# The output phase of the first token tiles woven into the third attention pair of the last block, with w_out in the place of the projection rows and weights

## The chip, the cores and the metric

One core of one Trainium2 chip runs the whole kernel. The metric is the device time of one execution in microseconds (us). Engines are named as in the profile: PE (TensorE), DVE (VectorE), ACT (ScalarE), POOL (GpSimd), SP (SyncE, which here issues the DMAs).

## The reference

One layer of a decoder trunk over 2048 tokens with 1024 channels, float32. The normalised input goes through one projection w_in whose columns feed three token mixers; their gated outputs are joined, projected by w_out and added to the input.

```python
h = rms_norm(x, norm_g) * (1 + scale) + shift
(ga_u, ga_v, ga_z, mb_q, mb_k, mb_v, mb_o, mb_z, mb_i, mb_f, sc_q, sc_k, sc_v, sc_z) = split(h @ w_in)
y_a = spatial_gating_branch(ga_u, ga_v, ...) * silu(ga_z)                  # 256 columns
h_b = mlstm_branch(conv(mb_q), conv(mb_k), mb_v, mb_i, mb_f)               # scan over 16 chunks of 128 tokens
y_b = sigmoid(mb_o) * rms_norm(h_b) * silu(mb_z)                           # 384 columns
y_c = stick_breaking_branch(rms_norm(sc_q), rms_norm(sc_k), sc_v) * silu(sc_z)   # 384 columns
out = x + gate * (concat([y_a, y_b, y_c]) @ w_out)

def stick_breaking_branch(q, k, v):        # 6 heads x 64, per block of 128 queries
    z = q @ k.T * scale
    log_not = where(strict, log_sigmoid(-z), 0.0)
    suffix = reverse_cumsum(log_not) - log_not
    a = where(strict, exp(log_sigmoid(z) + suffix), 0.0)
    return a @ v
```

The stick-breaking attention is causal, so a query tile i needs the i+1 key tiles up to itself. The mLSTM carries a state C from chunk to chunk.

## The kernel before, in words

Tokens are cut into 16 tiles of 128 and these into three blocks of 5, 5 and 6 tiles (BLOCKS). For a block the normalised, transposed rows hT stay in SBUF as a high and a low half (two float32r numbers whose sum is the float32), and every product with them is three matmuls: high by high, high by low, low by high. The weights wr are split in the same way; eight tiles of them make one set of 384 columns.

A block walks over three pairs of attention heads (p = 0, 1, 2 in the loop at the end of the kernel). For each pair `c_proj` projects q, k, v of the block's tiles, and `stick` runs the attention in units of up to four key tiles, each in four steps that lie one unit apart: `front` (two z matmuls, two sigmoids on ACT into bb and be, the running product of bb by a scan on DVE at L391, the product be at L395 on DVE and POOL in turn), `middle` (four PE transposes `at`, a cast on ACT at L408, the low half by a subtraction on DVE at L409), `back` (the av matmuls, L421) and `fin` (py, and the tile's 128 columns written to the DRAM scratch y_d). In the last block a pair is 44 units.

`interleave` runs a generator of fillers beside `stick`: other column sets of w_in, one `chunk` each (six tiles of 24 matmuls with 384 columns, 144 in all in the last block). They are bqk (q and k of the mLSTM), bg (its gates), cz, a (spatial gating) and bv (v of the mLSTM). In the last block pair 0 has bqk 0, bqk 1 and bg 0, pair 1 has bg 1, cz and a 0, pair 2 has a 1, and bv stands after the loop as `tail`; the gate scan `gating` and the mLSTM's chunk 0 (`first_chunk`) are mixed in. All results go to DRAM scratch (qkT_d, vb_d, gate_d, y_d).

What stands after `t0 += nb` is the output phase. It closes the pools of rows, weights and PSUM and opens its own: eight PSUM banks of five kinds, and w_out (`wst`, `wo`), which `split_wo` takes into high and low halves, eight tiles by two column halves. For each token tile i, `load` brings its parts back, `mlstm` does the chunk's scores, sums and the state's update (matmuls s, k, i, n, c and one DVE operation behind each), `mixed` normalises and gates, `turned` transposes y into yT, and `out_proj` does 48 matmuls `po` of 512 columns, multiplies by the gate (DVE, L967), adds x (POOL, L968) and stores. `weave` puts the steps of tile i+1 between the matmuls of tile i.

The order on each engine is made by the framework's scheduler from this program order and from priorities (`prio`; the sticks are ahead of the fillers by STK). Each engine then runs its own list in order, so an instruction that waits holds up all that stands behind it on its engine. The steps below speak of L296 to L298 (projection matmuls), L391, L395, L406 to L409, L421 (sticks), L640 (mLSTM weights by Exp on ACT), L863 and L864 (split of w_out), L914 (n), L957 to L959 (po).

Of the kernel before, what the change touches and what calls it, by code (L numbers as in the profile page):

```python
# [17 lines left out]
P = 128  # L18
# [14 lines left out]
def hybrid_block_kernel(ctx: ExitStack, tc: tile.TileContext, x, c, norm_g, w_ada, b_ada, w_in,  # L33
# [419 lines left out]
    def bqk_proj(t0, nb, half):  # L453
# [3 lines left out]
        for mm in range(3):  # L457
            m = half * 3 + mm
            for q in range(2):
# [9 lines left out]
                xb = tmp.tile([P, 64 * NBMAX + 3], F32, tag="xb", name=f"xb{m}_{t0}_{q}")  # L469
# [272 lines left out]
    def interleave(main, main_cost, side, side_cost):  # L742
# [14 lines left out]
        if side is not None:  # L757
            run(side)
# [48 lines left out]

    t0 = 0
    for b, nb in enumerate(BLOCKS):
# [7 lines left out]
        ]  # L817
        if b == 1:
            fillers[0] = (mix(fillers[0][0], 8, gate_gemv()), 3)
        if last:  # L820
            fillers[0] = (mix(fillers[0][0], 36, gating()), 3)
            fillers[1] = (mix(fillers[1][0], 14, first_chunk()), 3)
        for p in range(3):
# [4 lines left out]
            if p == 2 and not last:  # L828
                get_x(t0 + nb, 0)
                get_x(t0 + nb + 1, 1)  # L830
            interleave(stick(p, t0, nb), stick_cost(t0, nb), fillers[p][0], fillers[p][1] * chunk)
        tail = bv_proj(t0, nb)
        if last:
            run(tail)
        else:
# [9 lines left out]

    rs.close()
    lw.close()
    ps_ctx.close()
    pj_ctx.close()
    ld = ctx.enter_context(tc.tile_pool(name="ld", bufs=2))  # L850
    wk = ctx.enter_context(tc.tile_pool(name="wk", bufs=2, side="right"))
    wo_p = ctx.enter_context(tc.tile_pool(name="wo", bufs=1, side="right"))
    psS = ctx.enter_context(tc.tile_pool(name="psS", bufs=1, space=PSUM, side="right"))
    psN = ctx.enter_context(tc.tile_pool(name="psN", bufs=1, space=PSUM, side="right"))
    psK = ctx.enter_context(tc.tile_pool(name="psK", bufs=1, space=PSUM, side="right"))
    wo = [wo_p.tile([P, 2, D], F32R, tag=f"wo{k}", name=f"wo{k}") for k in range(KT)]

    wst = [ld.tile([P, 2, D], F32, tag=f"wst{kp}", bufs=1, name=f"wst{kp}") for kp in range(KT // 2)]

    def split_wo(k, n):  # L860
        cs = slice(n * 512, (n + 1) * 512)
        src = wst[k // 2][:, k % 2, cs]
        nc.scalar.copy(wo[k][:, 0, cs], src)  # L863
        (nc.gpsimd if k % 2 else nc.vector).tensor_tensor(wo[k][:, 1, cs], src, wo[k][:, 0, cs].bitcast(F32),  # L864
                                                          ALU.subtract)

    nds = {}
# [176 lines left out]
```

## Time and profile before

| what | us |
|---|---|
| median of the runs | 1480.47 |
| the profiled execution, its own time | 1480.27 |
| its span from first to last instruction | 1478.5 |
| last block, pair 0 (737 to 911 of the span) | 174 |
| last block, pair 1 (911 to 1084) | 173 |
| last block, pair 2 with bv (1084 to 1214) | 130 |
| output phase (1214 to the end) | 264.5 |

Times within the kernel are microseconds from the start of the span. The four stretches are cut where the sticks of a pair end on PE; a pair's `c_proj` lies at the stretch's start (that of pair 0 in part before it). Busy times of an engine are the union of its instructions; a busy PE is not PE at its peak, since matmuls are pipelined, so the pitch from one start to the next is used for its rate. PEclk is the share of TensorE's clock that was granted.

### The profile page before, as it was taken

The page shows a single profiled execution, that of the slowest core. Times are in us where ns is not written, and L with a number is a line of the kernel's source. Part 1 is how long each engine was busy: PE and PEld are TensorE (multiplying, and loading weights), DVE is VectorE, ACT ScalarE, POOL GpSimd, SP SyncE. Part 2 cuts the span into 40 slices and gives each one's busy share as a digit, 9 for nine tenths or more (in the row PEclk, how much of TensorE's full clock was granted, in tenths as well). Part 3 has the DMA queues.
Part 4 walks back from the last instruction along what each step waited for, and adds up shares of the span by engine and source line. Part 5 has one row for each costly group of instructions (what it writes and reads, how often), then busy time and mean ns, then how long its engine had stood idle before and what let it go on. Part 6 is the DMA issues. An engine that isn't in the chain of part 4 may idle for free.

```text
span 1478.5 us, 24942 instructions
## 1 busy us (share of the span) xinstructions
PE 1400.6 (95%) x8468; PEld 1302.7 (88%) x8468; DVE 1025.1 (69%) x1778; ACT 678.1 (46%) x1656; POOL 647.3 (44%) x1140
## 2 busy tenths in 40 slices
PE   4999999889999999999999899999999978999998
PEld 3789999879999999988899799989999867888887
DVE  6796555586894566588698975778778888444443
ACT  3365444444464355446367655555455655211210
POOL 4463554573443433455233353433344336534442
PEclk9999999999999999999999999999999998999999
DMA  9866766657635534625332343303432524555551
GB/s 319 305 203 216 249 213 190 207 187 240 203 114 194 175 114 137 213 98 184 114 117 78 104 148 131 104 27 107 158 100 74 190 89 128 185 152 159 171 156 57
DMA packets 187103, 233.19 MB, mean 158 GB/s; under 512 B 22714, under 2 KB 160344, under 8 KB 186976
## 3 DMA queue, kind: packets, MB, share of 16 engines
q1 hardware_dynamic: 186752, 231.59, 48.1%
q8 instruction: 67, 1.10, 0.3%
q14 instruction: 60, 0.49, 0.1%
q0 software_dynamic: 224, 0.02, 0.0%
HBM read 159.24 MB, written 72.31 MB: 157 GB/s over the span
## 4 chain that ended last, share of the span: by engine, by line
PE 68%; DVE 16%; DMA 5%; issue 4%; POOL 3%; ACT 3%; SPq 1%; DVEq 0%; POOLq 0%; ACTq 0%
DVE bb L391 6%; PE av L421 5%; PE pc L296 4%; PE pc L298 4%; PE at L406 4%; PE pc L297 4%; PE po L957 4%; PE po L959 3%; PE po L958 3%; PE pg L298 3%; PE pg L297 3%; PE pg L296 3%; PE pb L465 2%; PE pb L464 2%; PE z L378 2%
## 5 line engine op out<-in xcount | busy, mean ns | idle before, releaser
L391 DVE TENSOR_TENSOR_SCAN bb<-bb,bb 128x513 f32<-128x513 f32 x144 | 194.1, 1348 | 24.9 <-ACT bb L383 23.8
L395 POOL TENSOR_TENSOR be<-be,bb 128x512 f32<-128x512 f32 (+3 forms) x120 | 133.0, 1108 | 148.3 <-DVE bb L391 69.2
L409 DVE TENSOR_TENSOR aT<-at,aT 128x512 fp32r<-128x512 f32 (+3 forms) x240 | 142.7, 597 | 31.5 <-ACT aT L408 30.5
L421 PE MATMUL av<-aT,Vst 128*128 128x256 f32 x816 | 146.4, 296 | 15.0 <-DVE aT L409 12.1
L408 ACT CAST aT<-at 128x512 fp32r<-128x512 f32 (+3 forms) x240 | 127.1, 530 | 70.3 <-PE at L406 67.4
L383 ACT ACTIVATE bb<-z 128x512 f32<-128x512 f32 (+3 forms) x240 | 130.3, 544 | 54.5 <-PE z L379 44.2
L421 PEld LDWEIGHTS av<-aT,Vst 128*128 128x128 f32 x816 | 120.5, 192 | 27.0 <-DVE aT L409 19.2
L296 PE MATMUL pc<-wr,hT 128*128 128x384 f32 (+1 forms) x384 | 136.8, 358 | 7.6 <-DVE hT L290 5.7
L406 PE MATMUL at<-ident,be 128*128 128x128 f32 x816 | 132.8, 277 | 9.6 <-DVE Qst L351 4.5
L298 PE MATMUL pc<-wr,hT 128*128 128x384 f32 (+1 forms) x384 | 135.5, 353 | 1.6 <-DVE hT L290 1.5
L297 PE MATMUL pc<-wr,hT 128*128 128x384 f32 (+1 forms) x384 | 134.0, 349 | 0.0
L384 ACT ACTIVATE be<-z 128x512 f32<-128x512 f32 (+3 forms) x240 | 132.1, 550 | 0.0
L406 PEld LDWEIGHTS at<-ident,be 128*128 128x128 f32 x816 | 99.2, 142 | 19.0 <-DVE aT L409 8.0
L957 PE MATMUL po<-wo,yT 128*128 128x512 f32 x256 | 105.0, 410 | 0.3 <-ACT yT L946 0.3
L958 PE MATMUL po<-wo,yT 128*128 128x512 f32 x256 | 102.3, 400 | 1.9 <-DVE wo L864 1.9
L391 DVE TENSOR_TENSOR_SCAN bb<-bb 128x129 f32<-128x129 f32 (+3 forms) x96 | 86.9, 905 | 23.5 <-POOL bb L386 16.3
L959 PE MATMUL po<-wo,yT 128*128 128x512 f32 x256 | 101.5, 400 | 0.0
L382 POOL MEMSET bb<- 128x1 f32 x240 | 24.2, 101 | 168.4 <-DVE bb L391 118.1
L378 PE MATMUL z<-Kst,Qst 128*128 128x512 f32 (+3 forms) x240 | 92.7, 387 | 1.7 <-ACT be L384 1.6
L466 PE MATMUL pb<-hT,wr 128*128 128x320 f32 (+1 forms) x288 | 91.9, 324 | 2.4 <-DVE wr L190 2.4
L464 PE MATMUL pb<-hT,wr 128*128 128x320 f32 (+1 forms) x288 | 93.1, 324 | 0.6 <-DMA wr<-w_d 0.6
L465 PE MATMUL pb<-hT,wr 128*128 128x320 f32 (+1 forms) x288 | 92.2, 322 | 0.0
(272 smaller groups left out, 3905.2 us busy)
## 6 DMA issues: line engine op xcount, KB each, us to landing
wr<-w_d SPq DMA_DIRECT2D x160, 384.0 KB, 5.6
w_d<-wr SPq DMA_DIRECT2D x80, 384.0 KB, 3.5
wad<-in_w_ada_dram SPq DMA_DIRECT2D x8, 1024.0 KB, 6.8
xo<-in_x_dram SPq DMA_DIRECT2D x16, 512.0 KB, 3.7
out_dram<-o SPq DMA_DIRECT2D x31, 256.0 KB, 2.9
xt<-in_x_dram SPq DMA_DIRECT2D x15, 512.0 KB, 3.5
st<-in_w_in_dram SPq DMA_DIRECT2D x60, 128.0 KB, 3.7
wr<-w_d SPq DMA_DIRECT2D x16, 392.0 KB, 6.0
```

The source lines that it names most:

```text
L296: nc.tensor.matmul(ps, lhsT=hT[:, 0, k, cols], rhs=wt[k][:, 0, :W], start=k == 0, stop=False)
L297: nc.tensor.matmul(ps, lhsT=hT[:, 0, k, cols], rhs=wt[k][:, 1, :W], start=False, stop=False)
L298: nc.tensor.matmul(ps, lhsT=hT[:, 1, k, cols], rhs=wt[k][:, 0, :W], start=False, stop=k == KT - 1)
L384: nc.scalar.activation(be[:, :w], z[:, :w], AF.Sigmoid)
L391: nc.vector.tensor_tensor_scan(rev, rev, rev, carry.get((i, h), 1.0), ALU.mult, ALU.bypass)
L395: eng.tensor_tensor(be[:, :w], be[:, :w], bb[:, 1:w + 1], ALU.mult)
L406: nc.tensor.transpose(at[:, s, :], be[:, s * P:(s + 1) * P], ident)
L409: nc.vector.tensor_tensor(aT[:, :nb_, 1, :], at[:, :nb_, :], aT[:, :nb_, 0, :].bitcast(F32), ALU.subtract)
L421: nc.tensor.matmul(flat(av), lhsT=Vst[:, s0 + s, h, :], rhs=flat(aT[:, s]), start=(s0 + s == i), stop=(s0 + s == 0))
L957: nc.tensor.matmul(po, lhsT=yT[:, 0, k, :], rhs=wo[k][:, 0, cs], start=k == 0, stop=False)
L958: nc.tensor.matmul(po, lhsT=yT[:, 0, k, :], rhs=wo[k][:, 1, cs], start=False, stop=False)
L959: nc.tensor.matmul(po, lhsT=yT[:, 1, k, :], rhs=wo[k][:, 0, cs], start=False, stop=k == KT - 1)
```

## The change

The last block's fillers are dealt anew: pair 0 has bqk 0, bqk 1, bg 0 and bg 1, pair 1 has cz, a 0, a 1 and bv, four chunks each. Nothing of w_in is left for pair 2. Ahead of its sticks the pools of rows and weights are closed, w_out takes their place in SBUF, and the output phase itself, now a generator `output`, is the filler of the sticks of pair 2. `interleave` gives it up to 6 x 14500 ns of its own count of cost and, with `finish=False`, leaves the rest, which runs when the sticks have ended. Token tiles 0 to 5 and a part of 6 come before that end.

The buffers change with it. Until the sticks have ended the five kinds of PSUM tiles of `mlstm` share one bank (tag m) apart from the transposes, which use the sticks' `at` banks; afterwards s and n take the sticks' z banks and i the av bank. SBUF tiles of `mlstm`, `mixed`, `out_proj` and the staged w_out come from the six buffers t512 that the projections use too; gt, xt, vb use the buffers va and gu, xt, xb; the gate row lies in hscale. w_out is staged in pieces of 128 x 512. The computation is the same.

```diff
-    def interleave(main, main_cost, side, side_cost):
+    def interleave(main, main_cost, side, side_cost, finish=True):
...
-        if side is not None:
+        if side is not None and finish:
             run(side)
...
+    def open_out():
+        lw.close()
+        pj_ctx.close()
+        out_pools["o"] = ctx.enter_context(tc.tile_pool(name="psO", bufs=2, space=PSUM, side="right"))
+        out_pools["m"] = ctx.enter_context(tc.tile_pool(name="psM", bufs=1, space=PSUM, side="right"))
+        out_pools["ld"] = ctx.enter_context(tc.tile_pool(name="ld", bufs=2))
+        wo.extend(out_pools["ld"].tile([P, 2, D], F32R, tag=f"wo{k}", bufs=1, name=f"wo{k}") for k in range(KT))
+
+    def bank(kind, name):
+        pool, tag = {"s": (pz, "z"), "n": (pz, "z"), "i": (pav, "av")}.get(kind) if alone[0] and kind in "sni" else \
+            (pat, "at") if kind == "t" else (out_pools["m"], "m")
+        return pool.tile([P, 4, P], F32, tag=tag, name=name)
+
+    def load_wo(k, n):
+        st = t512(f"wst{k}_{n}")
+        nc.sync.dma_start(st, w_out[0, k * P:(k + 1) * P, n * 512:(n + 1) * 512])
+        return st
+
+    def split_wo(k, n, st):
+        cs = slice(n * 512, (n + 1) * 512)
+        nc.scalar.copy(wo[k][:, 0, cs], st)
+        (nc.gpsimd if k % 2 else nc.vector).tensor_tensor(wo[k][:, 1, cs], st, wo[k][:, 0, cs].bitcast(F32),
+                                                          ALU.subtract)
...
+    def weave(main, side, at):
+        for m, c in enumerate(main):
+            yield c
+            if m in at:
+                yield next(side, 0)
+        yield from side
+
+    def output():
+        load(0)
+        for k in range(KT):
+            split_wo(k, 0, load_wo(k, 0))
...
+        nc.sync.dma_start(gate_bc, ga_d.broadcast_to([P, D]))
+        mixed(0)
+        yield 0
+        yield from turned(0)
+        yield from out_proj(0, [0])
+        for k in range(KT):
+            split_wo(k, 1, load_wo(k, 1))
+        yield from chunk_ahead(1)
+        yield from out_proj(0, [1])
+        for i in range(1, NT):
+            if i + 1 < NT:
+                load(i + 1)
+                yield from weave(out_proj(i), chunk_ahead(i + 1), (0, 2, 4, 6, 8, 10, 13, 15))
+            else:
+                yield from out_proj(i)
...
+        if last:
+            fillers = [
+                (chain(bqk_proj(t0, nb, 0), bqk_proj(t0, nb, 1), bg_proj(t0, nb, 0), bg_proj(t0, nb, 1)), 4),
+                (chain(cz_proj(t0, nb), a_proj(t0, nb, 0), a_proj(t0, nb, 1), bv_proj(t0, nb)), 4),
+                None,
+            ]
...
+            if last and p == 2:
+                open_out()
+                rest = output()
+                interleave(stick(p, t0, nb), stick_cost(t0, nb), rest, 6 * 14500, False)
+                alone[0] = True
+                run(rest)
+                break
...
-        tail = bv_proj(t0, nb)
-        if last:
-            run(tail)
```

What the scheduler makes of it on PE is seen in the second half of pair 2's sticks. Before, the last matmuls of bv (pv) are followed by nothing but the sticks' own av, py, z and at:

```order
L296 MATMUL pv_14742<-wr_7_14595,hT 128x384
L297 MATMUL pv_14742<-wr_7_14595,hT 128x384
L298 MATMUL pv_14742<-wr_7_14595,hT 128x384
L421 MATMUL av_13_0_13885<-aT_13_0_12_13853,Vst 128x256 x2
L437 MATMUL py_12_13888<-fold,avt_12_1_13862 128x64
L378 MATMUL z_13_1_4_13995<-Kst,Qst 128x512
L379 MATMUL z_13_1_4_13995<-Kst,Qst 128x512
L406 MATMUL at_13_0_4_13907<-ident,be_13_0_4_13868 128x128 x4
L421 MATMUL av_13_0_13885<-aT_13_0_8_13882,Vst 128x256 x4
L406 MATMUL at_13_0_0_13953<-ident,be_13_0_0_13901 128x128 x4
```

Now, at about the same unit (query tile 13), po of the output phase and i, n of the mLSTM stand between them:

```order
L885 MATMUL i_14894<-C_14660,qk_4_14790 128x97 x4
L406 MATMUL at_13_1_12_14877<-ident,be_13_1_12_14829 128x128 x2
L939 MATMUL po_0_14801<-wo_13704,yT_14738 128x512
L937 MATMUL po_0_14801<-wo_13705,yT_14738 128x512
L938 MATMUL po_0_14801<-wo_13705,yT_14738 128x512
L939 MATMUL po_0_14801<-wo_13705,yT_14738 128x512
L937 MATMUL po_0_14801<-wo_13706,yT_14738 128x512
L938 MATMUL po_0_14801<-wo_13706,yT_14738 128x512
L939 MATMUL po_0_14801<-wo_13706,yT_14738 128x512
L421 MATMUL av_13_0_14746<-aT_13_0_0_14847,Vst 128x256 x4
L406 MATMUL at_13_1_8_14914<-ident,be_13_1_8_14868 128x128 x4
L378 MATMUL z_14_0_12_14975<-Kst,Qst 128x384
```

Of the 768 po matmuls 305 now stand ahead of the sticks' last one on PE, and 463 behind it.

On ACT the start of the output phase came behind the last cast of the sticks. Before:

```order
L408 CAST aT_15_1_0_14533<-at_15_1_0_14528 128x4x128
L425 COPY avs_15_1_14547<-av_15_1_14495 128x128
L439 COPY yc_15_14554<-py_15_14551 128x128
L640 ACT_TABLE_LOAD
L640 ACTIVATE wT_14927<-wT_14927,gT 128x128 x4
L640 ACTIVATE wT_15044<-wT_15044,gT 128x128 x4
L946 CAST yT_14849<-pty_0_14850 128x512
```

Now the same steps of tiles 1 and 2 stand between the sigmoids of the sticks' first query tiles:

```order
L838 CAST wo_13707<-wst_1_13931 128x512
L640 ACT_TABLE_LOAD
L640 ACTIVATE wT_13935<-wT_13935,gT 128x128 x4
L657 ACTIVATE sqo_14007<-hh_14006 128x384
L640 ACTIVATE wT_14163<-wT_14163,gT 128x128 x4
L924 CAST yT_14019<-pty_0_14020 128x512
L924 CAST yT_14019<-pty_1_14031 128x512
L408 CAST aT_10_1_0_14061<-at_10_1_0_14056 128x4x128
L384 ACT_TABLE_LOAD
L384 ACTIVATE be_11_0_0_14113<-z_11_0_0_14109 128x512
```

The table of Exp and that of Sigmoid are loaded in turn, 11 loads within pair 2 where there was none, and the sigmoid of the next stick unit (be_11_0_0) stands behind sqo, which needs the whole mLSTM step of tile 1, and behind yT.

## Rows read from the trace of the kernel before

**Rows 1.** The page's parts 1 and 2: busy us and share; tenths in 40 slices.

```profile
PE 1400.6 (95%) x8468; PEld 1302.7 (88%) x8468; DVE 1025.1 (69%) x1778; ACT 678.1 (46%) x1656; POOL 647.3 (44%) x1140
...
PE   4999999889999999999999899999999978999998
...
DVE  6796555586894566588698975778778888444443
...
PEclk9999999999999999999999999999999998999999
```

**Rows 2.** Busy time by stretch of the last block and the output phase.

```profile
core 0: us, PE busy (x) PEld busy (x) DVE busy (x) ACT busy (x) POOL busy (x), PEclk, DMA share, GB/s
737.00:911.00 174.00, 168.18 (x1053) 159.29 (x1052) 143.18 (x236) 108.58 (x233) 67.48 (x138) 1.00 0.35 113
911.00:1084.00 173.00, 170.87 (x1082) 163.74 (x1081) 131.81 (x215) 89.11 (x212) 68.92 (x137) 1.00 0.34 112
1084.00:1164.00 80.00, 79.11 (x502) 76.32 (x500) 63.71 (x111) 48.44 (x118) 32.66 (x76) 1.00 0.16 56
1164.00:1214.00 50.00, 38.83 (x239) 31.46 (x237) 45.05 (x57) 32.45 (x69) 18.82 (x36) 0.93 0.49 174
1214.00:1260.00 46.00, 40.07 (x238) 35.07 (x238) 36.30 (x60) 20.82 (x49) 29.10 (x29) 0.85 0.52 158
1260.00:1460.00 200.00, 199.31 (x1120) 169.77 (x1119) 93.93 (x174) 31.55 (x74) 90.11 (x97) 1.00 0.49 151
1460.00:1478.50 18.50, 13.78 (x63) 10.82 (x61) 4.78 (x9) 1.08 (x2) 1.35 (x2) 0.96 0.15 57
```

**Rows 3.** Waits of PE from 1164 to 1214, and from 1214 to 1260 (total, times, longest).

```profile
PE av L421 <- DVE aT L409: 6.9, 8, 1.6
...
PE n L914 <- DVE pT L645: 4.0, 2, 2.6
```

**Rows 4.** Busy time by stretch, the 20 us with the most DVE in pair 2.

```profile
1180.00:1200.00 20.00, 15.81 (x99) 13.50 (x100) 19.36 (x25) 13.44 (x28) 10.44 (x20) 0.91 0.45 150
```

**Rows 5.** Timeline of PE in a filler run: start, us, engine, line.

```profile
806.14 0.34 PE L466 MATMUL pb<-hT,wr 128*128 128x384 f32 x1
...
807.37 0.34 PE L464 MATMUL pb<-hT,wr 128*128 128x384 f32 x1
```

**Rows 6.** Groups by line on DVE from 1084 to 1214: busy us, mean ns, idle before.

```profile
L391 DVE TENSOR_TENSOR_SCAN bb<-bb,bb 128x513 f32<-128x513 f32 x32 | 43.0, 1343 | 3.8 <-ACT bb L383 3.6
L409 DVE TENSOR_TENSOR aT<-at,aT 128x512 fp32r<-128x512 f32 (+3 forms) x44 | 27.5, 630 | 6.2 <-ACT aT L408 6.2
L395 DVE TENSOR_TENSOR be<-be,bb 128x512 f32<-128x512 f32 (+3 forms) x22 | 14.3, 649 | 0.5
L391 DVE TENSOR_TENSOR_SCAN bb<-bb 128x385 f32<-128x385 f32 (+3 forms) x12 | 11.4, 951 | 2.7 <-POOL bb L386 1.6 <-POOL bb L382 1.1
...
L427 DVE TENSOR_TENSOR avt<-av,avs 128x128 f32<-128x128 f32 x11 | 3.0, 277 | 2.7 <-ACT avs L425 2.7
```

**Rows 7.** Busy time by stretch, instructions on the tile po alone.

```profile
1260.00:1460.00 200.00, 164.09 (x654) 118.03 (x653) 18.55 (x27) 1.00 0.49 151
1460.00:1478.50 18.50, 13.12 (x57) 10.10 (x55) 2.14 (x4) 0.96 0.15 57
...
1214.00:1260.00 46.00, 18.19 (x61) 12.41 (x62) 1.35 (x2) 0.85 0.52 158
```

**Rows 8.** Timeline of DVE at the start of the output phase.

```profile
1232.21 7.14 DVE L653 SCALAR_TENSOR_TENSOR sm<-nd,ex 128x4 f32<-128x4 f32 x1
```

**Rows 9.** Timeline of POOL at the same time.

```profile
1232.47 2.54 POOL L864 TENSOR_TENSOR wo<-wst,wo 128x512 fp32r<-128x512 f32 x2
1234.96 0.63 POOL L637 TENSOR_SCALAR_AFFINE_SELECT wT<-wT 128x512 f32<-128x512 f32 x1
1235.57 3.77 POOL L864 TENSOR_TENSOR wo<-wst,wo 128x512 fp32r<-128x512 f32 x3
```

**Rows 10.** Timeline of ACT at the start of the output phase.

```profile
1218.39 1.28 ACT L640 ACT_TABLE_LOAD   x1 [2.68 <-DMA wT<-m_d]
```

More of the change, by code (lines that the diff above doesn't have):

```diff
@@ new lines, in mixed, with turned @@
+    def mixed(i):
+        gt, y, xt = loaded[i][2:]
+        nc.gpsimd.tensor_tensor(y[:, 640:1024], y[:, 640:1024], gt[:, 384:768], ALU.mult)
+        if i > 0:
+            hh = t4(f"hh{i}", 96)
+            sq = t4(f"sqo{i}", 96)
+            sm = tmp.tile([P, 2, 4], F32, tag="smo", name=f"sm{i}")
+            normed(i, nds.pop(i), sm[:, 0, :], hh, sq, sm[:, 1, :], gt[:, 0:384], y[:, 256:640])
+    def turned(i):
+        y = loaded[i][3]
+        yT = out_pools["ld"].tile([P, 2, KT, P], F32R, tag="yT", name=f"yT{i}")
+        yTs[i] = yT
+        for hf in (0, 1):
+            pt = bank("t", f"pty{i}_{hf}")
+            for k in range(4):
+                kk = hf * 4 + k
+                nc.tensor.transpose(pt[:, k, :], y[:, kk * P:(kk + 1) * P], ident)
+            nc.scalar.copy(yT[:, 0, hf * 4:hf * 4 + 4, :], pt)
+            nc.vector.tensor_tensor(yT[:, 1, hf * 4:hf * 4 + 4, :], pt, yT[:, 0, hf * 4:hf * 4 + 4, :].bitcast(F32),
+                                    ALU.subtract)
+            yield 440
@@ L846, in hybrid_block_kernel @@
     rs.close()
-    lw.close()
     ps_ctx.close()
[L849 to L865, printed above, removed]
@@ L972, in chunk_ahead @@
-    def chunk_ahead(i):
-        yield from mlstm(i)
-        mixed(i)
-        yield
-        yield from turned(i)
-    def weave(main, side, at):
-        for m, _ in enumerate(main):
-            if m in at:
-                next(side, None)
-        run(side)
-    for kp in range(KT // 2):
-        if kp == 1:
-            load(0)
-        nc.sync.dma_start(wst[kp], w_out[0, kp * 256:(kp + 1) * 256, :].rearrange("(a p) f -> p a f", p=P))
-    load(1)
-    C0 = wk.tile([96, 4, 97], F32, tag="C", name="C0")
@@ L1002, in hybrid_block_kernel @@
-    nc.sync.dma_start(gate_bc, ga_d.broadcast_to([P, D]))
-    run(out_proj(0, [0]))
-    for k in range(KT):
-        split_wo(k, 1)
-    ahead = chunk_ahead(1)
-    for _ in range(6):
-        next(ahead)
-    run(out_proj(0, [1]))
-    run(ahead)
-    for i in range(1, NT):
-        if i + 1 < NT:
-            load(i + 1)
-            weave(out_proj(i), chunk_ahead(i + 1), (0, 2, 4, 6, 8, 10, 13, 15))
-        else:
-            run(out_proj(i))
 _INS = ["x", "c", "norm_g", "w_ada", "b_ada", "w_in", "ga_v_norm", "ga_ws", "ga_bs", "mb_conv_w", "mb_conv_b",
```

215 lines of the change are left out of this document (102 added, 113 removed).

## The prediction

> **What bounds the kernel now.** I read the page's first two parts, then a table of busy times by stretch, then the waits and the groups by line within the stretches that looked thin. On the page PE is busy for 95% of the span, and only two places of the second half fall below nine tenths: slices 32 to 34, which are the end of the last block and the start of the output phase, with PEclk falling there too [rows 1]. The table of stretches shows the same more sharply [rows 2]. From 737 to 1084 (pairs 0 and 1 of the last block) PE is busy for 339 of 347 us. From 1084 to 1164 (pair 2 while it has fillers) it still is. From 1164 to 1214 the fillers are used up and the sticks run alone: PE is busy for 38.8 of 50 us at a clock of 0.93, DVE for 45.1 of 50. There DVE bounds, and PE waits for the low halves that DVE makes, 6.9 us in 8 waits [rows 3]. From 1214 to 1260 the output phase starts with a chain (table load, Exp, pT, the mLSTM's matmuls, the split of w_out): PE is busy for 40.1 of 46 us, at a clock of 0.85. From 1260 on PE is full again.
>
> How much is lost in these 96 us? The idle time is 11.2 and 5.9 us [rows 2]. The clock's two levels are full (2.4 GHz) and half (1.2 GHz); a mean grant of 0.93 and 0.85 means 3.5 and 6.9 us of full clock missing. That is 27.5 us, 1.9% of the kernel, and all that closing the two gaps alone could give. It matters that the gaps aren't PE's own: the work that fills the first one comes from DVE too.
>
> **The sum, stretch by stretch.** PE's work is the same before and after, so I work out what each stretch lasts when the fillers are dealt anew. The sum is made against the profiled execution, 1480.27 us, which is 0.2 us below the median of the runs.
>
> *Pair 0, one chunk more (bg 1).* A filler matmul starts every 0.176 us (seven pitches in 1.23 us [rows 5]), so 144 of them are 25.3 us. PE's idle time in that stretch, 174 less 168.2 = 5.8 us [rows 2], can hide some of it: between +19.5 and +25.3. It lies where the sticks ran alone, which is where the added chunk goes, but some of those waits belong to the gate scan; I take +22.
>
> *Pair 1, one chunk more (bg 1 goes, a 1 and bv come).* The same 25.3 us, with 2.1 us of idle time to hide in: +23.2 to +25.3, taken as +24.
>
> *Pair 2: sticks with 6.35 token tiles (305 of 768 po matmuls at 48 a tile) in place of two chunks.* Before, it lasted 130 us. For PE: in the steady output phase 654 po in 200 us [rows 7] make 13.6 tiles, 14.7 us a tile, so 6.35 tiles are 93 us; the sticks' own part follows from pair 1, 173 us less 2 of idle, less three chunks (76) and the projection of the pair (25.3), 70 us. PE needs 163 us. For DVE: the sticks take 43.0 + 11.4 (44 scans), 27.5, 14.3 and 3.0, together 99 us [rows 6]. The output phase took 36.3 + 93.9 + 4.8 = 135 us of DVE for 16 tiles [rows 2]; shared evenly the 6.35 tiles get 54 us; if the 9.65 tiles left behind take only the steady 6.9 us each (93.9 by 13.6), pair 2 gets 68, for the start with the splits of w_out falls into it. So DVE has 153 to 168 us, taken as 160. DVE is now the fuller engine, about equal to PE. How full can it be when both must be fed? It was 0.80 from 1084 to 1164, 0.82 in pair 0, 0.90 when the sticks had PE for themselves [rows 2], and 0.97 in its best 20 us [rows 4]. I take 0.85, between the mixed stretches and the one where it bounds: 160 / 0.85 = 188 us. The lowest that I can see is PE's 163, the highest 168 / 0.80 = 210.
>
> *The start-up.* It doesn't vanish, it moves into the first sixth of pair 2. The orders on ACT show it: the wT, sqo and yT steps of tile 1 stand ahead of the next stick's sigmoid, with a table load of 1.28 us [rows 10] before and after. What waits behind them on ACT are sigmoids, behind these the scans on DVE, behind those PE's at and av. PE has only the po of column half 0 and a few sticks to cover it. In the old start DVE was busy for 36.3 of 46 us, 0.79; the same DVE work at 0.85 would take 42.7, so the start costs 3.3 us more than the stretch's mean. Pair 2: 191 us, +61. ACT itself has room (it was busy for 48.4 + 32.5 of pair 2's 130 us [rows 2]), so I charge the 11 table loads at nothing beyond this; if that cover is gone they cost up to 11 x 1.28 = 14 us, inside the upper bound.
>
> *The rest of the output phase.* 463 po are left, 9.65 tiles at 14.7 us = 141.6, and the end: the last 57 po took 18.5 us where the steady pace gives 17.4, so 1.1. That is 142.7 in place of 264.5: -121.8.
>
> *Loads and pools.* w_out's 4 MB came during the sticks before and comes during the projection's end and the first sticks now; the tiles wo lie where rows and weights were, so the casts begin when the projection's last matmul has read hT. That is within the start-up's price. The buffer xb, one column wider, costs nothing that PE or DVE would see.
>
> Sum: 22 + 24 + 61 - 121.8 = -14.8, so 1480.3 - 14.8 = **1466 us** (rounded), 1.0% faster. Both ends: 19.5 + 23.2 + 33 - 121.8 = -46 gives 1434; 25.3 + 25.3 + 83 - 121.8 = +12 gives 1492.
>
> **The rivals.**
> (1) *The weave packs DVE nearly full.* If pair 2 runs DVE at its best share, 0.97, it lasts 165 us, just over PE's need. Then 22 + 24 + 35 - 121.8 = -41: 1439 us, faster by 2.8%. For it: it is a share DVE has reached [rows 4], and po waits for no DVE step, so PE is never short. Against: that share came without fillers, and each of the six tiles brings a dozen DVE steps that wait for PE, ACT or POOL in between. The line of 2% lies at a pair 2 of 176 us, a share of 0.91.
>
> (2) *POOL and DVE stand in each other's way in pair 2* (slower). At 1232 a DVE operation on four columns lasted 7.14 us, exactly while POOL ran three splits and selects back to back [rows 8, 9]. In pair 2 POOL gets the sticks' work (at most 51.5 us) and 6.35 tiles at (29.1 + 90.1 + 1.4) / 16 = 7.5 us, together 99 us [rows 2]. DVE's operations with both inputs in SBUF are the scans and be, 69 us [rows 6], and some of the output's 60, of which I take a third. If the two never overlap, 188 us are filled by them alone; at the share of 0.90 this is 209, and with the start 212: 22 + 24 + 82 - 121.8 = +6, 1486 us. It decides from where POOL and these operations together exceed DVE's own sum. Against: from 1164 to 1214 DVE reached 0.90 beside a POOL that was busy for 0.38, and I saw no second wait of that length.
> The Trainium skill (SBUF — State Buffer, section "SBUF: two separate sides") says that a DVE operation with two SBUF inputs and a POOL operation that reads SBUF take an exclusive lock in turn and the other blocks wholly. By that rule the time would be this rival's 1486; the trace agrees for the 7.14 us and doesn't say how often it happens.
>
> (3) *The remaining tiles run slower than before*, since wT, pT, kw, nd, hh, sq and both o now share six buffers, and k and c one bank. If each of the 9.65 tiles pays one wait such as the longest of PE for pT, 2.6 us [rows 3], that is +25: 1491 us. Against: after the sticks s, n and i have banks of their own again, and the order puts 16 or more po between two users of one bank.
>
> That the change doesn't do what it says I leave out: the order shows po between the sticks.
>
> **How the numbers follow.** Forecast (pair 2 between 177 and 203 us) 0.55, rival 1 0.20, rival 2 0.16, rival 3 0.09. The range of 8 in 10 reaches nearly to rival 1's time below and past rival 2's above: 1438 to 1490 us. A difference of 2% (29.6 us) is about what a measurement of this kernel can tell from no change. Faster by more than that, under 1450.7: nearly all of rival 1 and a small tail of the forecast, 0.23. Slower by more, over 1509.9: only rivals 2 and 3 together or a worse one, 0.04. Within 2%: 0.73.
>
> **What would show it.** In the new profile, pair 0 should last 194 to 199 us and pair 1 196 to 198; pair 2 about 191 with DVE at 0.84 or so and PE visibly idle in its first 50 us; the tiles behind it 14.7 us each, with no gap like that of 1214 to 1260. DVE over 0.91 in pair 2 would be rival 1; many DVE operations stretched beside POOL, rival 2; a tile over 16 us behind the sticks, rival 3. I am wrong if pair 2 lasts under 176 or over 205 us, or if pairs 0 and 1 take much less than a chunk's 25 us each.

## The result and the profile after

The changed kernel takes 1529.99 us (median of 4 runs, 1527.80 to 1531.03) against 1480.43 us: a ratio of 1.0334, 95% interval 1.0314 to 1.0354. It is slower by 49.6 us, where 1466 us was forecast, with a range to 1490 and a chance of 0.04 for slower by over 2%. The profiled execution took 1529.46 us with a span of 1527.7. One of the four runs of the kernel before took 3433.93 us and is not in the ratio.

First the page's parts 1 and 2 of the changed kernel, the lines that answer to [rows 1] (busy us and share; tenths in 40 slices).

```profile
PE 1425.7 (93%) x8468; PEld 1320.7 (86%) x8468; DVE 1032.3 (68%) x1778; ACT 693.3 (45%) x1666; POOL 653.0 (43%) x1140
...
PE   5999999799999999998999999999996898998987
...
DVE  6796545677983665887788756788566777844442
...
PEclk9999999999999999999999999999997899999998
```

PE has as many instructions as before and is busy for 25 us longer; the same matmuls ran at a lower clock (a mean grant of 0.966 over the span, 0.982 before). Apart from the kernel's first slice, the thinnest place is now slices 31 and 32 (1146 to 1222 us), with digits 6 and 8 and PEclk at 7 and 8, and from there to the end eights stand among the nines, where PE was full behind its thin place in [rows 1].

Now the table by stretch that answers to [rows 2]: pair 0, pair 1 and pair 2 of the last block, each from its first scan to that of the next (pair 2 to its last av), and the rest. Under it is pair 2 of the kernel before, cut at the same points.

```profile
core 0: us, PE busy (x) PEld busy (x) DVE busy (x) ACT busy (x) POOL busy (x), PEclk, DMA share, GB/s
738.80:932.40 193.60, 191.09 (x1193) 183.76 (x1191) 143.50 (x241) 112.15 (x239) 74.88 (x149) 1.00 0.36 120
932.40:1130.40 198.00, 196.24 (x1224) 188.36 (x1224) 140.13 (x246) 96.68 (x239) 71.11 (x149) 1.00 0.34 112
1130.40:1344.80 214.40, 182.19 (x1024) 154.22 (x1025) 162.82 (x227) 110.81 (x224) 106.12 (x147) 0.89 0.34 106
1344.80:1527.70 182.90, 163.10 (x838) 135.21 (x836) 76.81 (x139) 25.64 (x63) 63.80 (x68) 0.93 0.36 116
```

```profile
1086.20:1213.40 127.20, 115.13 (x722) 105.37 (x721) 106.96 (x164) 78.80 (x182) 51.03 (x111) 0.97 0.28 98
```

Pair 0 takes 193.6 us (174 before), pair 1 198.0 (173), pair 2 214.4 (127.2), and the rest 182.9, where before it took 265.1 (1213.4 to 1478.5). Together +19.6 + 25.0 + 87.2 - 82.2 = +49.6 us, against 49.2 between the two profiled executions. So nothing is lost outside these four stretches. Two of the four terms came as forecast. Pair 2 was to grow by 61 us and grew by 87, and the rest was to shrink by 121.8 and shrank by 82.2: 26 and 40 us of miss.

The rest shows a wait that the kernel before hardly had. The longest row among the waits of PE behind the sticks (total, times, longest):

```profile
PE pty L923 <- POOL y L662: 14.0, 6, 3.5
```

The longest row among the waits of SP's queue in the same stretch:

```profile
SPq L850 <- PE c L898: 56.8, 6, 11.5
```

The transposes of y wait for the last product of the normalisation, 14.0 us in 6 waits; from 1260 to 1460 the kernel before had one such wait, of 0.7 us. And SP stands 56.8 us with the load of v (vbl, line 850) at the head of its queue until the matmul c of an earlier tile has read the buffer; before, from 1260 to 1460, that was 12.8 us in 7 waits. The load of the next tile's wT, with which its chain begins, stands behind vbl in this queue.

What one such wait does is seen on PE's timeline (start, us, engine, line):

```profile
1433.37 0.88 PE L923 MATMUL pty<-ident,y 128*128 128x128 f32 x6 [1.50 <-POOL y L662]
1434.54 0.50 PE L937 MATMUL po<-wo,yT 128*128 128x512 f32 x1 [0.29 <-ACT yT L924]
...
1435.72 0.63 PE L939 MATMUL po<-wo,yT 128*128 128x512 f32 x1
1436.15 0.63 PE L937 MATMUL po<-wo,yT 128*128 128x512 f32 x1
...
1438.28 0.63 PE L939 MATMUL po<-wo,yT 128*128 128x512 f32 x1
...
1439.91 0.40 PE L938 MATMUL po<-wo,yT 128*128 128x512 f32 x1
1440.15 0.39 PE L939 MATMUL po<-wo,yT 128*128 128x512 f32 x1
```

PE is idle for 1.50 and 0.29 us. The first po behind that still start 0.23 to 0.34 us apart, then they start every 0.43 us for 3 us, until the pitch is 0.24 again. From 1435.7 to 1438.7 the granted clock was 0.50, the half clock. Seven po at 0.43 in place of 0.24 us are 1.3 us, so the wait is paid about twice. Over the stretch the idle time is 182.9 - 163.1 = 19.8 us, and a mean clock of 0.93 is 12.8 us of full clock missing.

### The profile page after: what moved, and what is told of

Read it like the earlier page. It is cut to its first block, busy times and chain, and to the rows that moved or that the text cites. A ratio compares the mean times of both kernels' runs of the same rounds, so it can differ in the third digit from the quotient of the medians.

```text
span 1527.7 us, 24957 instructions
## 1 busy us (share of the span) xinstructions
PE 1425.7 (93%) x8468; PEld 1320.7 (86%) x8468; DVE 1032.3 (68%) x1778; ACT 693.3 (45%) x1666; POOL 653.0 (43%) x1140
## 5 line engine op out<-in xcount | busy, mean ns | idle before, releaser
L937 PE MATMUL po<-wo,yT 128*128 128x512 f32 x256 | 110.0, 430 | 1.2 <-ACT yT L924 1.2
L938 PE MATMUL po<-wo,yT 128*128 128x512 f32 x256 | 106.5, 416 | 2.6 <-DVE wo L839 2.5
L939 PE MATMUL po<-wo,yT 128*128 128x512 f32 x256 | 102.4, 408 | 0.0
```

The costliest lines, as they stand in the source:

```text
L937: nc.tensor.matmul(po, lhsT=yT[:, 0, k, :], rhs=wo[k][:, 0, cs], start=k == 0, stop=False)
```

## The experiments

The ratio is to the kernel before on the same chip; "pair 2" and "rest" are the stretches as above, with the number of po matmuls in each.

| run | what | us | ratio (95%) | pair 2, po | rest, po |
|---|---|---|---|---|---|
| (after) | the change | 1530.0 | 1.0334 (1.0314 to 1.0354) | 214.4, 288 | 182.9, 480 |
| e1_step | seven steps a tile | 1537.7 | 1.0381 (1.0361 to 1.0401) | 225.8, 322 | 178.5, 446 |
| e2_own | own buffers behind the sticks | 1508.9 | 1.0186 (1.0169 to 1.0204) | 219.9, 288 | 157.0, 480 |
| e3_both | both of these | 1519.7 | 1.0262 (1.0247 to 1.0277) | 232.5, 321 | 157.2, 447 |
| e4_first | first chunk woven into po | 1530.8 | 1.0338 (1.0323 to 1.0354) | 217.1, 309 | 183.9, 459 |
| f1_deal | kernel before, new deal alone | 1498.3 | 1.0121 (1.0092 to 1.0150) | 105.8, 0 | 264.7, 768 |
| f4_own_none | own buffers, no po woven | 1505.4 | 1.0169 (1.0149 to 1.0189) | 123.9, 0 | 250.3, 768 |
| f5_own_spread | own buffers, start spread out | 1508.2 | 1.0184 (1.0163 to 1.0204) | 192.1, 228 | 184.6, 540 |
| f2_own_bv | own buffers, bv in pair 2 | 1515.9 | 1.0236 (1.0216 to 1.0255) | 224.9, 240 | 181.4, 528 |
| g1_nochain | own buffers, no mLSTM in tiles 1 to 6 | 1470.9 | 0.9937 (0.9908 to 0.9965) | 180.7, 306 | 154.3, 462 |
| g3_nopo | own buffers, 6 po a tile in tiles 0 to 6 | 1478.6 | 1.0002 (0.9989 to 1.0015) | 191.6, 40 | 153.9, 434 |
| g2_deal323 | kernel before, chunks 3, 2, 3 | 1482.2 | 1.0018 (1.0008 to 1.0028) | 141.7, 0 | 278.7, 768 |
| h2_early5 | the same, fillers dealt faster | 1478.4 | 0.9999 (0.9987 to 1.0010) | 153.6, 0 | 265.7, 768 |

### What slows the tiles behind the sticks: e1_step, e2_own, e3_both

Two causes stood open. The tiles wT, pT, kw, nd, hh, sq and both o share six buffers (theory A). And the change puts a yield behind c, so that a tile's side has eight steps where the kernel before had seven, and the transposes come three po later (theory B).

```diff
# e1_step, and in e3_both
             CT[0] = Cn
-            yield 330
...
         mixed(i)
-        yield 0
+        yield 330
```

> The weave of the output phase gets back the seven steps a tile that the kernel before had: c and the normalisation are one step again, so the transposes of y stand three po steps earlier in the program. Theory A (six shared buffers make the chain of the mLSTM late): almost nothing changes, the tiles behind the sticks stay at 18 us or more, 1515 to 1532 us. Theory B (the eighth step moves the transposes to just ahead of the po that need them): these tiles come back to 14.7 to 15.5 us, 1485 to 1500 us. Theory C (neither: the banks that s, n, k and c share, or the loads): 1525 to 1535 us.

```diff
# e2_own, and in e3_both
+    OWN = {"wT": ("bb", 4), "o": ("be", 3), "nd": ("aT", 3)}
+    def tbuf(name):
+        kind = name.rstrip("0123456789_")
+        if alone[0] and kind in OWN:
+            tag, n = OWN[kind]
+            return stk.tile([P, D if tag == "aT" else 512], F32, tag=tag, bufs=n, name=name)[:, 0:512]
+        return t512(name)
...
-        return t512(name)[:, 0:4 * n].rearrange("p (h e) -> p h e", h=4)
+        return tbuf(name)[:, 0:4 * n].rearrange("p (h e) -> p h e", h=4)
...
-                    o = t512(f"o{i}_{n}")
+                    o = tbuf(f"o{i}_{n}")
```

> Behind the sticks wT, nd and o get buffers of their own, those that the sticks leave free; pT, kw, hh and sq alone keep the six. Theory A (sharing): the tiles behind the sticks take 14.7 to 15.5 us, 1487 to 1500 us. Theory B (the eighth step): still 17.5 us or more a tile, 1515 to 1530 us. Theory C (banks or loads): 1525 to 1535 us.

> Seven steps and own buffers together. Theories A and B: the tiles behind the sticks take 14.7 us, as before, and the whole is at 1484 to 1492 us, the lower of the two that one part alone gives. Theory C (banks that s, n, k and c share, or the loads): no gain, 17.5 us or more a tile, 1520 us or more. Pair 2 is not touched by the buffers: 213 us, or a few less by the seven steps.

Own buffers bring 21 us, the seven steps cost 8 to 11. The stretch table of the run with own buffers, pair 2 and the rest:

```profile
1130.20:1350.10 219.90, 183.90 (x1014) 155.67 (x1015) 163.47 (x226) 116.90 (x238) 107.81 (x151) 0.88 0.34 107
1350.10:1507.10 157.00, 151.72 (x848) 127.53 (x847) 72.41 (x140) 22.61 (x51) 60.70 (x65) 1.00 0.41 131
```

PE's wait for y in its rest:

```profile
PE pty L932 <- POOL y L662: 0.3, 1, 0.3
```

And SP's wait with vbl there:

```profile
SPq L850 <- PE c L907: 19.2, 4, 6.4
```

For the same 480 po the rest takes 157.0 us in place of 182.9. PE's wait for y falls from 14.0 to 0.3 us, the clock is 1.00, and SP's wait with vbl falls from 56.8 to 19.2 us although vbl itself kept its buffers. From the sticks' end to the last po the ten tiles take 15.2 us each (1350.1 to 1502.0) in place of 17.8 (1344.8 to 1522.7): 2.6 us a tile. Theory A holds and B falls: with seven steps alone (e1_step) PE waits even longer for y behind the sticks, where a tile takes 18.7 us (9.3 tiles from 1356.8 to 1530.7):

```profile
PE pty L922 <- POOL y L662: 19.1, 6, 7.2
```

None of the three times fell where a theory had it. The times expected of A for e2_own and e3_both were too low, since they credited the buffers with what pair 2 loses; e1_step, at 1537.7 us, is above all three of its ranges (its pair 2 is 11 us longer with 34 po more, its rest only 4 us shorter); and in e3_both a tile behind the sticks takes 16.4 us and not 14.7. Pair 2 of e2_own is 5.5 us longer than that of the changed kernel with as many po, which isn't explained. Which of the three tiles needed its own buffers was not tried apart. That the seven steps are worse even with own buffers (pair 2 longer by 12.6 us with 33 po more, and nothing saved behind) was measured and isn't explained.

### What the deal and the weave cost: f1_deal, f4_own_none

```diff
# f1_deal, in the kernel before
+        if last:
+            fillers = [
+                (chain(bqk_proj(t0, nb, 0), bqk_proj(t0, nb, 1), bg_proj(t0, nb, 0), bg_proj(t0, nb, 1)), 4),
+                (chain(cz_proj(t0, nb), a_proj(t0, nb, 0), a_proj(t0, nb, 1), bv_proj(t0, nb)), 4),
+                (None, 0),
+            ]
...
-        tail = bv_proj(t0, nb)
-        if last:
-            run(tail)
-        else:
+        if not last:
+            tail = bv_proj(t0, nb)
```

> The kernel before with the new deal of fillers alone: four chunks in pair 0, four in pair 1, none in pair 2, and the old output phase behind, with its own buffers and loads. It prices the refill. Theory F (the two chunks were nearly half hidden in pair 2 and cost a full 23 us each in pairs 0 and 1): pairs 0 and 1 take 44 to 49 us more, pair 2 with the sticks alone takes 105 to 115 us in place of 130 (DVE's 99 us at a share of 0.86 to 0.94), 1500 to 1512 us. Rival (pair 2 alone is as short as DVE's 99 us at 0.97): pair 2 about 102 us or less, 1490 to 1498 us.

```diff
# f4_own_none, on top of e2_own
-                interleave(stick(p, t0, nb), stick_cost(t0, nb), rest, 6 * 14500, False)
+                interleave(stick(p, t0, nb), stick_cost(t0, nb), rest, 0 * 14500, False)
```

> The changed kernel with own buffers behind the sticks and nothing of the output phase woven in beyond the steps that cost no time in its account (the loads and splits of column half 0): pair 2 is the sticks alone and 16 tiles run behind it. It prices the weave against the run with own buffers, 1508.9 us. Theory G (the weave wins the fill of pair 2, some 30 us, but its start costs 20 us there): pair 2 takes 105 to 115 us, the start and the tiles 270 to 285 us, 1510 to 1525 us. Rival (woven tiles cost as much in pair 2 as behind it): 1500 to 1510 us.

Pair 2 with the sticks alone, in f1_deal:

```profile
1132.20:1238.00 105.80, 77.35 (x453) 60.51 (x451) 98.71 (x128) 69.10 (x152) 46.27 (x89) 0.94 0.25 87
```

Pair 2 and the rest of f4_own_none:

```profile
1129.40:1253.30 123.90, 85.93 (x474) 68.18 (x475) 112.74 (x137) 83.73 (x187) 62.01 (x103) 0.88 0.23 66
1253.30:1503.60 250.30, 245.15 (x1388) 207.62 (x1386) 117.81 (x229) 38.99 (x89) 103.42 (x112) 1.00 0.47 143
```

The deal alone costs 18 us. Its two chunks take 19.3 and 24.8 us more in pairs 0 and 1 (193.3 and 197.8 us there) and free only 127.2 - 105.8 = 21.4 us in pair 2: there half of them had been hidden. By the stretches theory F holds. The median, 1498.3 us, lies between the two forecasts, 1.7 us under F's range and 0.3 us above the rival's. The profiled execution, 1504.70 us, is the longest of its four: its span is 24 us longer than before, where the medians differ by 18. Two of these 6 us lie ahead of pair 0; where the others lie isn't known.

The weave brings nothing, and so the rival holds against theory G. With own buffers and not one po in pair 2 the kernel takes 1505.4 us; with six tiles woven in, 1508.9, and the two intervals overlap. The six tiles cost 219.9 - 123.9 = 96.0 us in pair 2, 16.0 each, and save 250.3 - 157.0 = 93.3 us behind it, 15.6 each. The idle time of PE in pair 2 says it most simply: 123.9 - 85.9 = 38.0 us without po, 219.9 - 183.9 = 36.0 us with 288 of them. The tiles came beside the idle time, not into it. The clock gives nothing back either: its mean in pair 2 is 0.88 in both runs.

### The start: e4_first, f5_own_spread, f2_own_bv

ACT's timeline of the changed kernel shows what the start does to the sticks (in brackets: idle before, and what ended it):

```profile
1155.70 0.61 ACT L383 ACTIVATE bb<-z 128x512 f32<-128x512 f32 x1
1156.20 1.66 ACT L838 CAST wo<-wst 128x512 fp32r<-128x512 f32 x3
1165.27 1.97 ACT L838 CAST wo<-wst 128x512 fp32r<-128x512 f32 x3 [7.42 <-DMA wst<-in_w_out_dram]
1167.31 1.28 ACT L640 ACT_TABLE_LOAD   x1
1169.61 1.28 ACT L640 ACTIVATE wT<-wT,gT 128x128 f32<-128x128 f32 x4 [1.02 <-POOL wT L637]
1179.51 0.52 ACT L657 ACTIVATE sqo<-hh 128x384 f32<-128x384 f32 x1 [8.63 <-DVE hh L656]
...
1192.84 0.60 ACT L384 ACTIVATE be<-z 128x512 f32<-128x512 f32 x1
```

No sigmoid runs from 1156.2 to 1192.8. The casts of column half 1 wait 7.4 us for a load, the square of tile 1 waits 8.6 us for its chain, and the sticks' sigmoids stand behind both in ACT's queue. In two stretches of 20 us at that place PE and DVE are both idle for a good part:

```profile
1160.00:1180.00 20.00, 13.97 (x52) 10.65 (x51) 10.75 (x16) 4.91 (x9) 7.40 (x7) 0.67 0.26 84
1180.00:1200.00 20.00, 16.60 (x86) 14.67 (x87) 9.16 (x16) 8.37 (x17) 7.47 (x11) 0.76 0.34 108
```

```diff
# e4_first
-        yield from chunk_ahead(1)
-        yield from out_proj(0, [1])
+        yield from weave(out_proj(0, [1]), chunk_ahead(1), range(8))
# f5_own_spread, on top of e2_own
             split_wo(k, 1, load_wo(k, 1))
-        yield from chunk_ahead(1)
-        yield from out_proj(0, [1])
+            yield 700
+        yield from weave(out_proj(0, [1]), (c + 2500 for c in chunk_ahead(1)), range(8))
```

> The first woven mLSTM chunk (tile 1) no longer stands by itself ahead of the po of column half 1 of tile 0, it is woven into them, one step for each. Theory D (the 20 us of pair 2 in which PE ran s, k, i, n, c one behind the other at the half clock are lost for want of cover): pair 2 takes 195 to 203 us in place of 213, 1510 to 1520 us, and PE is busy for more than 36 of the 40 us around the place where it was for 30.6. Theory E (the chain through DVE, ACT and POOL sets the start, whatever stands beside it on PE): pair 2 at 208 to 214 us, 1524 to 1532 us. The tiles behind the sticks stay at 18.5 us by either.

> Own buffers as in the run with 1508.9 us, and the start of the output phase is spread over the sticks: a stick step after each split of column half 1, and the first chunk of the mLSTM woven into the po of tile 0, each of its steps charged 2.5 us more in the account, so that sticks stand between them. Some 1.8 tiles fewer are woven in, which costs nothing by itself. Theory H (the bunch of splits and of the first chunk stands in ACT's and DVE's queues ahead of the sigmoids and scans and stops the sticks for 34 us): ACT's wait of 8.6 us for the first sqo goes or no longer stops the sticks, PE is busy for over 36 of the 40 us around 1160 to 1200, 1488 to 1499 us. Theory E (the chain of the start takes its time wherever it stands): 1503 to 1512 us.

The first edit changes nothing (1530.8 us): PE is busy for 31.5 of these 40 us, and pair 2 takes 217.1 us, so theory D falls; E has the time, though pair 2 is 3 us over its range. The second does what it is for: ACT's wait for the first hh falls to 2.2 us, and in the same two stretches DVE is full.

```profile
1160.00:1180.00 20.00, 16.78 (x94) 13.43 (x94) 20.00 (x23) 13.94 (x29) 12.91 (x18) 0.95 0.17 57
1180.00:1200.00 20.00, 16.01 (x99) 13.13 (x97) 19.96 (x30) 12.95 (x30) 11.78 (x19) 0.91 0.28 86
```

PE gets to 32.8 of these 40 us from 30.6, less than the 36 expected, and the time is 1508.2 us where 1508.9 was: pair 2 is shorter by 27.8 us with 60 po fewer, the rest longer by 27.6 us with 60 po more. So the stall at the start is real, it can be taken away, and it isn't what the weave is lost by. Theory H has its mechanism right and its price wrong; E has the price.

```diff
# f2_own_bv, on top of e2_own
-                (chain(cz_proj(t0, nb), a_proj(t0, nb, 0), a_proj(t0, nb, 1), bv_proj(t0, nb)), 4),
+                (chain(cz_proj(t0, nb), a_proj(t0, nb, 0), a_proj(t0, nb, 1)), 3),
...
+    def late():
+        yield from bv_proj(t0, nb)
+        open_out()
+        yield from output()
...
-                interleave(stick(p, t0, nb), stick_cost(t0, nb), rest, 6 * 14500, False)
+                interleave(stick(p, t0, nb), stick_cost(t0, nb), rest, chunk + 5 * 14500, False)
```

> Own buffers as in the run with 1508.9 us, and the chunk bv goes back from pair 1 into the first part of pair 2, ahead of the output phase; five tiles are woven in place of six. Theory F (a chunk costs 25 us in a pair whose PE is full and less in pair 2): pair 1 is 23 to 25 us shorter and pair 2 at most 12 us longer, 1494 to 1503 us. Rival (pair 2 has no room left, the chunk costs there what it cost in pair 1): 1506 to 1516 us.

1515.9 us: pair 1 gives 21 us back, but pair 2 takes 224.9 us with one tile fewer. With the output phase woven in there is no room for the chunk. The rival holds.

### Which part of a woven tile costs: g1_nochain, g3_nopo

A woven tile is 48 po matmuls and a chain (mLSTM, normalisation) through ACT, DVE, POOL and back to PE. Each kernel takes one of the two away.

```diff
# g1_nochain, on top of e2_own
     def mlstm(i):
+        if i <= 6:
+            for _ in range(5):
+                yield 0
+            return
...
-        if i > 0:
+        if i > 6:
             hh = t4(f"hh{i}", 96)
# g3_nopo, on top of e2_own
             for k in range(KT):
+                if i <= 6 and k < KT - 1:
+                    yield 3 * 512 / 2.2
+                    continue
```

> Own buffers as in the run with 1508.9 us, but tiles 1 to 6 leave the mLSTM and its normalisation out (they take the part of y that tile 0 takes, and the state C is not carried through them); their gate product, transposes, casts, po and evacuations stay, at the same places of the weave. Theory K (the woven tile's chain through DVE, ACT and POOL stands among the sticks' steps in the same queues and keeps PE idle as long as with the sticks alone, 36 to 38 us): without it the idle time of pair 2 falls under 20 us, its clock rises over 0.94, and it takes 160 to 180 us in place of 219.9. Theory L (po itself, in front of the sticks' matmuls in PE's queue, makes the sticks late): only the matmuls left out go, some 3 us a tile, idle time stays over 28 us, pair 2 takes 190 to 205 us.

> Own buffers as in the run with 1508.9 us, but of the 48 po matmuls of each of tiles 0 to 6 only the last 6 are left (out then holds a part of the product there); all chains, transposes and evacuations stay. 252 po go from pair 2, 59 us of PE at the full clock. Theory K (the chains set the length): pair 2 shortens by less than 30 us, 190 us or more, with PE idle for 70 us or more. Theory L (PE's work simply adds up): it shortens by 50 us or more, to 170 us or less.

Pair 2 without the chains, in g1_nochain:

```profile
1129.30:1310.00 180.70, 154.68 (x826) 126.25 (x827) 132.88 (x163) 98.60 (x205) 83.11 (x120) 0.94 0.42 124
```

Pair 2 without most po, in g3_nopo:

```profile
1128.30:1319.90 191.60, 134.76 (x784) 112.34 (x785) 164.44 (x229) 116.09 (x241) 110.64 (x151) 0.80 0.41 127
```

With the two runs from above that makes a table of pair 2:

| | no po | po |
|---|---|---|
| no chains | 123.9 us | 180.7 us (306 po) |
| chains | 191.6 us (40 po) | 219.9 us (288 po) |

The chains alone make pair 2 longer by 67.7 us, 11.3 a tile, and then DVE is busy for 164.4 of 191.6 us, a share of 0.86. The po added to them cost another 28.3 us: 248 po at a pitch of 0.24 us are 60 us, so about half of them is hidden and half isn't. By their numbers theory K is nearer: without most po pair 2 loses only 28 us (it said under 30, L over 50), though PE's idle time grew to 56.8 us and not over 70. And g1_nochain is 0.7 us past K's range and well short of L's: 180.7 us, with a clock of 0.94 and an idle time of 26.0 us where K wanted under 20. Neither part sets the length by itself.

How the po lengthen pair 2 is seen in the waits of DVE, which is as busy with them (163.5 us) as without (164.4) and is idle for 56.4 us in place of 27.2. The row that grows most is the wait for the sticks' cast on ACT, first with the po (e2_own), then without most of them (g3_nopo):

```profile
DVE aT L409 <- ACT aT L408: 18.7, 14, 6.3
DVE aT L409 <- ACT aT L408: 3.2, 6, 0.9
```

Two more waits of the sticks, for the sigmoid bb and for the copy of av, grow from 0.7 to 8.7 us together. The longest wait for that cast in the changed kernel itself shows what stands in front of it:

```profile
1286.04 0.53 DVE L395 TENSOR_TENSOR be<-be,bb 128x384 f32<-128x384 f32 x1
1294.13 0.39 PE L939 MATMUL po<-wo,yT 128*128 128x512 f32 x1
1294.37 1.03 PE L406 MATMUL at<-ident,be 128*128 128x128 f32 x8
1295.00 0.59 ACT L408 CAST aT<-at 128x512 fp32r<-128x512 f32 x1 [4.65 <-PE at L406]
1295.62 0.69 DVE L409 TENSOR_TENSOR aT<-at,aT 128x512 fp32r<-128x512 f32 x1 [6.22 <-ACT aT L408]
```

The last product be ahead of the eight transposes ended at 1286.6. From 1288.4 on PE ran 23 po, and the transposes started behind the last of them, at 1294.4. Until then ACT was idle but for a few short casts and copies, and DVE from 1289.4 on. So the place of the po in PE's queue is what delays the sticks, at least in the waits that can be followed. A kernel with the transposes ahead of the po was not run.

### The deal the other way: g2_deal323, h2_early5

If projection chunks hide well in pair 2, a third one there should pay, in the kernel before.

```diff
# g2_deal323, in the kernel before
         if last:
+            fillers[1] = (chain(bg_proj(t0, nb, 1), cz_proj(t0, nb)), 2)
+            fillers[2] = (chain(a_proj(t0, nb, 0), a_proj(t0, nb, 1)), 2)
...
-            fillers[1] = (mix(fillers[1][0], 14, first_chunk()), 3)
+            fillers[1] = (mix(fillers[1][0], 14, first_chunk()), 2)
# h2_early5: as g2_deal323, but bv goes with them and the tail's bv goes
+            fillers[2] = (chain(a_proj(t0, nb, 0), a_proj(t0, nb, 1), bv_proj(t0, nb)), 5)
```

> The kernel before with the deal moved the other way: three chunks in pair 0, two in pair 1, three in pair 2 (a 0 goes there), the output phase as it was. From the run with the new deal alone: a chunk in pair 1 costs 25 us, two chunks in pair 2 cost 21.5 us together. Theory M (projection chunks fill the sticks' idle time, there are 12 us of it left in pair 2): pair 1 is 23 to 25 us shorter, pair 2 12 to 18 us longer, 1468 to 1475 us. Rival (pair 2 is full with two): pair 2 22 to 27 us longer, 1478 to 1485 us.

> The kernel before with three chunks in pair 0, two in pair 1 and three in pair 2, as in the run that took three, two and three, but the three chunks of pair 2 are dealt faster, so that the last projection matmul comes about a quarter of the sticks ahead of their end, where the kernel before has it, and the loads of the output phase can start there. Theory N (in that run the 13 us won in pair 2 were lost again because the last filler held weights and rows until the sticks' end and the loads came late: 26.7 us from there to the first po in place of 13.5): that distance is 12 to 16 us again, pair 1 stays at 148 us and pair 2 takes 140 to 147 us, 1466 to 1474 us. Rival (pair 2 without fillers at its end gives the gain back): pair 2 over 150 us, 1477 to 1483 us.

The stretches of g2_deal323: pair 1, pair 2, from the sticks' end to the first po, the rest.

```profile
910.70:1058.80 148.10, 142.23 (x914) 134.17 (x913) 115.22 (x174) 83.27 (x188) 57.00 (x117) 1.00 0.29 95
1058.80:1200.50 141.70, 138.51 (x881) 131.76 (x881) 118.44 (x205) 85.41 (x209) 60.81 (x131) 1.00 0.27 88
1200.50:1227.20 26.70, 16.27 (x80) 13.86 (x80) 8.30 (x14) 8.64 (x20) 7.14 (x8) 0.62 0.93 297
1227.20:1479.20 252.00, 241.35 (x1355) 205.37 (x1353) 128.89 (x229) 44.98 (x107) 111.06 (x120) 0.99 0.46 142
```

Pair 1 gives 25 us and pair 2 takes 14.5, as theory M has it, but the time, 1482.2 us, is the rival's. The sticks now end 13 us earlier and the first po comes at the same time as before (1227.2 and 1227.0): PE waits for loads of the output phase, 5.6 us for qk and 3.1 us for C, at a DMA share of 0.93. In the program these loads stand behind the last filler. In h2_early5 the fillers end earlier; the first po comes 7.9 us behind the sticks, and pair 2 takes 153.6 us, 26.4 more than before. It is level with the kernel before (0.9987 to 1.0010), as the rival said. With its fillers dealt so, a third chunk costs in pair 2 what it saves in pair 1. No version that does the whole computation beat the kernel before.

## Why the prediction failed

**Pairs 0 and 1: right.** +22 and +24 were forecast, +19.6 and +25.0 measured, each near an end of its range.

**"DVE has 153 to 168 us, taken as 160": right.** It was busy for 162.8 us. Some 12 of these are operations that ran longer than before, so the agreement is in part luck. Rival 2, POOL and DVE in each other's way, shows in these groups: the 32 long scans took 1436 ns each against 1343 [rows 6], the 15 long be products on DVE 875 ns against 720 in the same pair of the kernel before, and, against the kernel before's output phase, the eight splits of w_out on DVE 1291 ns against 793 and the two hh products of six tiles 1098 and 996 against 742 and 856. The scans don't owe it to the woven tiles: with the sticks alone (f1_deal) they took 1448 ns. DVE's operations with an input from PSUM kept their time (aT 679 and 672 ns, yT 676 and 686). Rival 1, DVE packed nearly full, fell: its share was 0.76. The Trainium skill (SBUF — State Buffer, section "SBUF: two separate sides") has it that a DVE operation with two SBUF inputs and a POOL operation that reads SBUF block each other wholly. The trace agrees in which groups ran longer; that POOL ran beside each of them is not shown. The price that the rival worked out, 212 us for pair 2 and 1486 us in all, didn't come about in that way: the 12 us lie inside DVE's busy time.

**"160 / 0.85 = 188" and with the start 191: this step failed.** It took the larger of two needs, DVE's 160 us at a share of 0.85 against PE's 163, and counted the other as hidden. For the chains alone it came out, 191.6 us at 0.86 in the run with 40 po, but by luck in part, since that run holds the long stall of the start, which the sum priced at 3.3 us. What it left out is that the po don't lie under that time. For its rival 1 the text argued that "po waits for no DVE step, so PE is never short", and it left out what waits behind the po: they stand in PE's queue between the sticks' matmuls, and an at or av that comes later makes a cast later and DVE idle. Half of their time came on top. Then the sum is 123.9 + 67.7 + 28.3 = 219.9 us with own buffers, 214.4 in the changed kernel, past the 205 at which the text called itself wrong. The four numbers are shown, and the place in the queue by DVE's waits, 23.5 of the 29 us that it is idle for longer. The sum also took PE's need, 163 us, at the full clock: at the mean grant of 0.89 some 24 us of full clock are missing in these 214.4 us, and PE was busy for 182.2.

**"The start costs 3.3 us more": wrong in size, of little weight.** The sigmoids stood still for 36 us; spreading the start took the stall away and moved the time by nothing that can be measured.

**"The rest: 14.7 us a tile, -121.8": this step failed, and by more.** Rival 3 says how. It was priced at 2.6 us a tile, 1491 us, and given a chance of 0.09; measured are 2.6 us a tile (17.8 against 15.2). That the two figures agree is luck: the rival took one wait of PE for pT, and measured are waits for y, 1.4 us a tile, with 1.3 us a tile of missing clock. Its reason was the six shared buffers, and the run with own buffers, which leaves k and c in their one bank, takes the 2.6 us away. The argument against it, 16 or more po between two users of a bank, was about the banks and didn't touch the buffers. Of the 40 us of miss 26 are this. Some 5 come from the cut alone (17 po at 14.7 / 48 us): the 305 po of the prediction were counted to the sticks' last py, at 1349.8, and this table cuts at the last av, with 17 po in between, so that they belong to pair 2's miss. The remaining 8 or 9 are tiles at 15.2 where 14.7 was taken, and a longer end. The text's own mark for this rival, a tile over 16 us, is what the profile shows.

**The whole.** Step by step from 1480: the deal +18 (f1_deal), the open start with the new buffers +7 (f4_own_none), the six woven tiles +3.5, within what the runs differ by (e2_own), and the shared buffers +21 (after). The 2% that the text took as the least a measurement can tell is too much: the intervals of the table are 0.2 to 0.6% wide. The prediction saw the gap in pair 2 as room for PE's work. In [rows 2] the sticks alone left PE idle for 11 of 50 us, and projection chunks do use that: two of them cost 21.4 us there instead of 44. Output tiles don't. Behind the sticks a tile's chain is hidden under po, and PE is busy for 245.2 of 250.3 us; in pair 2 the chain goes through DVE, the fuller engine there (0.91 without one po), and the po hold up the steps that feed DVE. Without the chains, the po with their transposes, casts and evacuations are hidden by a quarter: 306 of them, 73 us at 0.24, cost 56.8 us.

## What to carry to other kernels

Idle time of one engine was room here for projection matmuls, about half hidden, and hardly for work that also passes through the engine that is nearly full. Ask of a filler not only what it waits for, but what waits behind it in the queue. Where filler and main work each run through the same queues, price neither as the larger of two needs: take one of them out, then the other, and read all four lengths. When tiles move from pools of their own into a shared one, write down for each which tile had its buffer last and who reads that, and look for loads that stand behind such a wait in the DMA queue.

## What was not expected of the hardware

A wait of PE of 1.5 us was followed by about as much again in clock: 3 us at a grant of 0.50, with the po at a pitch of 0.43 us in place of 0.24. Behind the sticks 14.0 us of waits for y came with 12.8 us of missing full clock, and both went together when the buffers were parted (clock 0.93 to 1.00). And a gap can keep its size while the work in it more than doubles: PE's idle time in pair 2 was 38.0 us at 85.9 us of work and 36.0 us at 183.9.
